# A hybrid decoder layer on one core: three rows of the tokens' fourth factor are loaded into the places of the blocks' transposed rows

## The chip, the core and the metric

The kernel runs on one core of one Trainium2 chip. Its metric is the device time of one execution in microseconds (us). Three runs of the kernel before gave 2222.38, 2222.5 and 2226.02 us; their median is 2222.5 us. The profile shows one further execution, with a time of its own.

## The reference

One decoder layer over 2048 tokens and 16 meta tokens, model width 1024, all in float32: an input projection, two groups of heads side by side (attention in a sliding window of 128, and a gated linear attention in chunks), an output projection, a layer norm, a SwiGLU feed-forward of width 2816, and a second layer norm.

```python
def hybrid_mixer(h, w_in, b_in, ...):
    proj = jnp.einsum('bld,de->ble', h, w_in) + b_in
    ...
    o_s = sliding_window_gqa(...)
    ...
    o_g = rms_norm(o_g, gla_norm_g).reshape(B, L, GLA_WIDTH) * jax.nn.silu(r_g)
    o = jnp.concatenate([o_s, o_g], axis=-1)
    return jnp.einsum('ble,ed->bld', o, w_out)

def reference(...):
    ...
    for l in range(DEPTH):
        mix = hybrid_mixer(h, ...)
        h = layer_norm(ALPHA * h + mix, ln1_g[l], ln1_b[l])
        ffn = swiglu(h, w_ffn_gate[l], w_ffn_up[l], w_ffn_down[l])
        h = layer_norm(ALPHA * h + ffn, ln2_g[l], ln2_b[l])
    return h[:, N_META:]
```

## The kernel before

Every matrix product of float32 values is made of three matmuls in a shorter format: an operand is split into a high part (a copy on ACT, L185) and a low part (a subtraction on DVE or POOL, L186), and TensorE (PE) adds high x high, low x high and high x low (`matmuls`, L197). `split_into` and `matmuls` are helpers, so many different steps of the program share these three lines; the tiles' names tell them apart.

The tokens are worked on in four blocks of 512 (s = 0 to 3). Each block is projected, mixed (attention and gated linear attention) and then given its output projection by the class `Mixed`. That class has the steps the change touches:

- `x(qd)`, four times per block, is a quarter of the output projection (256 columns). Its weights come as two loads of 1 MB, `hl_o{s}_{qd}_0` and `_1` (L221), and they go in turn through four places (tag "whl"). For each of the block's four groups of 128 tokens (n = 0 to 3) 24 matmuls write `po{s}_{n}_{qd}` into a PSUM bank, of which this step has two (tag "mm"). DVE then adds the bank to the residual row `yo{s}_{n}` (L930) and so frees the bank. The four residual rows are loaded by L915, 512 KB each, into seven places (tag "yo"): two blocks need eight, so `yo3_3`, the last row of the last block, takes the place of `yo2_0`, the first row of the block before, and can be loaded only when that row has been read for the last time.
- `y` is the layer norm of the rows and their store (L936). `z` transposes the finished rows on PE, eight transposed tiles per block, `nt{s}_{k}`, of four 128x128 transposes each (L943). ACT copies each one to a tile `ntr{s}_{k}` (L950, 256 KB, three places, tag "nt" in the pool `op_`), and it is stored to the scratch tensor `n_scT` (L952). The last transpose that reads `yo2_0` is the first of `nt2_7`.

The feed-forward works with sums of blocks ("factors") and seven products. The tokens' factors of the first half of the tokens are named by `EARLY = ["b11", "t2", "t1", "b21"]`, and those after it. `combine` makes the sums from `n_scT` and stores them in `t_sc` (its tiles `cb` take the places "nt" too); `make` loads a factor's four rows and splits them. A row is 128x512, 256 KB. `b11` and `t2` are made early, in the last block's steps; `t1` and `b21` are made once the projection's pools are closed (`ops.update({f: make(f, 0) ...})`). Their rows `r_t1..` and `r_b21..` go through three places, tag "mk" in the pool `hop1`, which they share with the rows of the next factor `t3`.

All of these steps end in one stretch, from some 876 us of the profile on: the matmuls of the last block's output projection (`po3_..`), the transposes of block 2 (`nt2_..`) and the loads of `t1`, `b21` and `t3` are laid out there by `FIRST_PRODUCTS`. The order of instructions on each engine is not written by hand: the framework's scheduler sets it with a simulation of its own when the kernel is built, from which buffers it believes to be free when. Every engine then runs its list strictly in order. SP issues nearly all DMAs, in its own order, on one hardware queue (q1), and with eight semaphores in turn: an issue also waits until the DMA eight issues before it has landed. In what follows, "SP" is this issuing engine.

Of the kernel before, what the change touches and what calls it, by code (L numbers as in the profile page):

```python
# [8 lines left out]
F32 = mybir.dt.float32  # L9
# [5 lines left out]
P = 128  # L15
# [108 lines left out]
def body(ctx, tc, t, seq):  # L124
# [11 lines left out]
    HT = TF // 2  # L136
# [47 lines left out]
    def split_into(hi, lo, src, lo_eng=None, hold=lambda i: i):  # L184
        hold(nc.scalar.activation(hi, src, AF.Copy))  # L185
        hold((lo_eng or nc.vector).tensor_tensor(lo, src, r32(hi), op=ALU.subtract))  # L186
# [18 lines left out]
    def staging(name):  # L205
        return wpool.tile([P, D], F32, tag="x", name=name, bufs=3)
# [68 lines left out]
    with ExitStack() as c1:  # L275
# [436 lines left out]
        for s in range(NSB):  # L712
# [5 lines left out]
            for what in WINDOW_STEPS.split():  # L718
                op, k = what[0], int(what[1])
# [26 lines left out]
    EARLY = ["b11", "t2", "t1", "b21"]  # L746
# [4 lines left out]
    pools = {}  # L751

    def quarter(tb, kh, th, k, n):

        c = tb * TF + th * HT
        k0 = kh * (KT // 2) + k
        return n_scT[c // TB][:, k0 : k0 + n, c % TB : c % TB + HT]
# [42 lines left out]
    def make(f, tb):  # L800

        if f in FIRST:
            x = hb.tile([P, 2, KT // 2, HT], F32R, tag="h16", name=f"h_{f}_{tb}", bufs=2)
        else:
            pool = pools["hop1" if f in EARLY else "hop3" if f == "b22" else "hop2"]
            x = pool.tile([P, 2, KT // 2, HT], F32R, tag=f"h_{f}", name=f"h_{f}_{tb}", bufs=1)
        if f in FIRST and tb == 0:
            for k in range(0, KT // 2, 2):
                raw = staging(f"r_{f}{tb}_{k}").rearrange("p (k q) -> p k q", q=HT)
                if f in SOURCE:  # L810
                    nc.sync.dma_start(raw, quarter(tb, *SOURCE[f], k, 2))
                else:
                    i, j = COMBINED[f]
                    nc.sync.dma_start(raw, t_sc[tb][i, :, k : k + 2, j])
                split_into(x[:, 0, k : k + 2], x[:, 1, k : k + 2], raw, nc.vector)
            return x
        if tb > 0:

            for k in range(0, KT // 2, 2):
                raw = pools["hop4"].tile([P, D], F32, tag="x3", name=f"r_{f}{tb}_{k}", bufs=4).rearrange("p (k q) -> p k q", q=HT)  # L820
                if f in SOURCE:
                    held(nc.sync.dma_start(raw, quarter(tb, *SOURCE[f], k, 2)))
                else:
                    i, j = COMBINED[f]
                    held(nc.sync.dma_start(raw, t_sc[tb][i, :, k : k + 2, j]))
                split_into(x[:, 0, k : k + 2], x[:, 1, k : k + 2], raw, nc.vector if k else nc.gpsimd)
            return x
        for k in range(KT // 2):
            raw = pools["hop1"].tile([P, HT], F32, tag="mk", name=f"r_{f}{tb}_{k}", bufs=3)
            if f in SOURCE:  # L830
                nc.sync.dma_start(raw, quarter(tb, *SOURCE[f], k, 1)[:, 0, :])
            else:
                i, j = COMBINED[f]
                nc.sync.dma_start(raw, t_sc[tb][i, :, k, j])
            split_into(x[:, 0, k], x[:, 1, k], raw, nc.vector if k % 2 else nc.gpsimd)
        return x
# [3 lines left out]
    op_ = c1.enter_context(tc.tile_pool(name="go", bufs=1, side="right", reuse_waits="tile"))  # L840
# [362 lines left out]
    def start_ffn(n):  # L1203

        if n < 2:
            ops[FIRST[n]] = make(FIRST[n], 0)
        elif n == 2:
            st = staging("a11_first")
            nc.sync.dma_start(st, t["w_gu"][0, 0, 0])
            hl = early["pa11"] = wpool.tile([P, 2, D], F32R, tag="whl", name="pa11_first", bufs=4)  # L1210
            split_into(hl[:, 0, :], hl[:, 1, :], st)
        else:
            hl = early.pop("pa11")
            early["b11"] = [mm_psum(f"b11{m}_first") for m in range(2)]
            for m, pt in enumerate(early["b11"]):
                matmuls(pt, ffn_terms(hl, ops["b11"], m))
# [33 lines left out]
    fp = hops.enter_context(tc.tile_pool(name="fp", bufs=1, reuse_waits="tile"))  # L1250
    pools["hop1"] = hops1.enter_context(tc.tile_pool(name="hop1", bufs=1, reuse_waits="tile"))
    ops.update({f: make(f, 0) for f in EARLY if f not in ops})


# [81 lines left out]
    raw, factors = {}, {}  # L1336
# [258 lines left out]
    AFTER, f = {}, None  # L1595
    for what in FIRST_PRODUCTS.split():
        if what[0] == "P":
            f = EARLY[int(what[1])]
# [4 lines left out]
    def finish_mixing(f):  # L1603
        for what in AFTER.get(f, ()):
            take(what.lower(), last if what[0] in "YZ" else mix)
        if f != BEFORE[-1]:
            return
        c1.close()
        pools["psB"] = hops.enter_context(tc.tile_pool(name="psB", bufs=1, space=PSUM, reuse_waits="tile"))
        for n in ("hop2", "hop3"):  # L1610
            pools[n] = c2.enter_context(tc.tile_pool(name=n, bufs=1, side="right", reuse_waits="tile"))
        ops.update({f: make(f, 0) for f in ("t3", "t4", "b22")})
        pools["hop4"] = hops1.enter_context(tc.tile_pool(name="hop4", bufs=1, reuse_waits="tile"))
# [132 lines left out]
```

## Time and profile before

| | |
|---|---|
| median of three runs | 2222.5 us (2222.38 to 2226.02) |
| the profiled execution's own time | 2216.87 us |
| its span | 2215.0 us |
| PE busy | 2158.8 us, 97% |
| DVE, POOL, ACT busy | 65%, 55%, 38% |

The profile is of one execution. Its own time is 1.87 us above its span and 5.63 us below the median of the three runs; a change of time is worked out inside this execution and then set on the median. PE is the busy engine, so a time is gained or lost where PE stands still, or where its clock is lowered: PEclk in a table of stretches is the granted clock as a share of the full 2.4 GHz, and 0.50 is 1.2 GHz. In a timeline a bracket at the end of a row tells how long the engine stood before that instruction and which instruction released it.

### The profile page before, as it was taken

The page shows a single profiled execution, that of the slowest core. Times are in us where ns is not written, and L with a number is a line of the kernel's source. Part 1 is how long each engine was busy: PE and PEld are TensorE (multiplying, and loading weights), DVE is VectorE, ACT ScalarE, POOL GpSimd, SP SyncE. Part 2 cuts the span into 40 slices and gives each one's busy share as a digit, 9 for nine tenths or more (in the row PEclk, how much of TensorE's full clock was granted, in tenths as well). Part 3 has the DMA queues.
Part 4 walks back from the last instruction along what each step waited for, and adds up shares of the span by engine and source line. Part 5 has one row for each costly group of instructions (what it writes and reads, how often), then busy time and mean ns, then how long its engine had stood idle before and what let it go on. Part 6 is the DMA issues. An engine that isn't in the chain of part 4 may idle for free.

```text
span 2215.0 us, 31559 instructions
## 1 busy us (share of the span) xinstructions
PE 2158.8 (97%) x11564; PEld 1858.7 (84%) x11564; DVE 1444.7 (65%) x2285; ACT 838.1 (38%) x1477; POOL 1220.2 (55%) x951
## 2 busy tenths in 40 slices
PE   8899999999999999999999999999999999999998
PEld 7788888889999998878888888788888888888886
DVE  6556645466745576368998567766656555876787
ACT  5544644544352443342223223322223242232443
POOL 4656645655634071368776666776666536432433
PEclk9999999999999999999999999999999999999999
DMA  8987773576786787766352318523232299655463
GB/s 296 316 277 252 254 268 127 193 277 226 290 294 225 253 310 244 274 252 219 130 196 103 131 45 286 189 101 109 90 125 81 98 360 330 219 185 177 166 232 124
DMA packets 181918, 460.92 MB, mean 208 GB/s; under 512 B 16978, under 2 KB 65011, under 8 KB 167684
## 3 DMA queue, kind: packets, MB, share of 16 engines
q1 hardware_dynamic: 176804, 452.26, 58.1%
q10 hardware_dynamic: 4960, 6.65, 0.8%
q8 instruction: 92, 1.51, 0.3%
q14 instruction: 62, 0.51, 0.1%
HBM read 306.67 MB, written 152.17 MB: 207 GB/s over the span
## 4 chain that ended last, share of the span: by engine, by line
PE 85%; DMA 4%; DVE 4%; POOL 3%; issue 2%; ACT 2%; SPq 0%; DVEq 0%; POOLq 0%; ACTq 0%
PE t L197 20%; PE d L1377 18%; PE b L197 14%; PE pu L197 13%; PE po L197 6%; PE pv L197 4%; PE lp L1151 2%; PE oa L680 1%; DMA r_t<-t_sc 1%; DMA cb<-n_scT 1%; DMA x<-x 1%; PE s L627 1%; PE s L628 1%; ACT pr L643 1%; PE nt L943 1%
## 5 line engine op out<-in xcount | busy, mean ns | idle before, releaser
L1377 PE MATMUL d<-B,A 128*128 128x512 f32 x1848 | 419.0, 389 | 0.0
L1377 PEld LDWEIGHTS d<-B,A 128*128 128x128 f32 x1848 | 346.9, 188 | 72.0
L197 PE MATMUL t<-h_t,ps 128*128 128x512 f32 x1584 | 367.9, 390 | 3.2 <-DMA ps<-parts_ps 2.4
L197 PEld LDWEIGHTS t<-h_t,ps 128*128 128x128 f32 x1584 | 296.8, 188 | 65.8 <-issue 2.1
L197 PE MATMUL pu<-h,hl_u 128*128 128x512 f32 (+1 forms) x1032 | 249.3, 389 | 7.2 <-ACT gr L692 4.5
L197 PE MATMUL b<-h_b,pa 128*128 128x512 f32 x1032 | 241.9, 390 | 0.3 <-ACT pa L185 0.2
L197 PEld LDWEIGHTS b<-h_b,pa 128*128 128x128 f32 x1032 | 193.7, 188 | 41.3 <-ACT pa L185 0.7
L186 POOL TENSOR_TENSOR pa<-a,pa 128x1024 fp32r<-128x1024 f32 x62 | 160.7, 2591 | 103.8 <-ACT pa L185 103.8
L197 PEld LDWEIGHTS pu<-h,hl_u 128*128 128x128 f32 x1032 | 184.0, 197 | 38.8 <-ACT gr L692 5.1
L197 PE MATMUL po<-hl_o,msh 128*128 128x256 f32 x1024 | 198.3, 289 | 4.8 <-DVE yo L930 3.1
L186 DVE TENSOR_TENSOR A<-rA,A 128x1024 fp32r<-128x1024 f32 (+1 forms) x78 | 117.2, 1527 | 119.7 <-ACT A L185 119.7
L197 PEld LDWEIGHTS po<-hl_o,msh 128*128 128x128 f32 x1024 | 162.1, 191 | 6.6 <-DVE yo L930 4.2
L185 ACT ACTIVATE A<-rA 128x1024 fp32r<-128x1024 f32 (+1 forms) x78 | 78.6, 1042 | 215.2 <-PE d L1377 200.2
L197 PE MATMUL po<-hl_o,msl 128*128 128x256 f32 x512 | 146.3, 286 | 0.0
L1647 DVE TENSOR_TENSOR u<-u,t 128x512 f32<-128x512 f32 x132 | 89.3, 680 | 84.2 <-PE t L197 84.1
L197 PE MATMUL b<-h_b,ps 128*128 128x512 f32 x528 | 126.9, 396 | 2.9 <-ACT h_b L185 2.8
L197 PE MATMUL t<-h_t,pa 128*128 128x512 f32 x528 | 123.8, 390 | 0.0
L1573 POOL TENSOR_TENSOR a<-a,a 128x1024 f32<-128x1024 f32 x42 | 121.2, 2887 | 1.6
L197 PEld LDWEIGHTS b<-h_b,ps 128*128 128x128 f32 x528 | 100.8, 191 | 25.0 <-ACT h_b L185 3.2
L197 PEld LDWEIGHTS t<-h_t,pa 128*128 128x128 f32 x528 | 99.0, 188 | 20.4
L185 ACT ACTIVATE ps<-a 128x1024 fp32r<-128x1024 f32 x63 | 66.7, 1059 | 123.4 <-PE t L197 81.9
L185 ACT ACTIVATE pa<-a 128x1024 fp32r<-128x1024 f32 x62 | 65.8, 1060 | 110.1 <-PE t L197 52.7
(355 smaller groups left out, 4292.0 us busy)
## 6 DMA issues: line engine op xcount, KB each, us to landing
hl_u<-w_u SPq DMA_DIRECT2D x42, 1024.0 KB, 6.7
a<-w_gu SPq DMA_DIRECT2D x84, 512.0 KB, 4.2
rA<-a_sc SPq DMA_DIRECT2D x66, 512.0 KB, 4.6
w<-w_d SPq DMA_DIRECT2D x50, 512.0 KB, 5.5
hl_o<-w_o SPq DMA_DIRECT2D x24, 1024.0 KB, 8.0
hT_sc<-h SPq DMA_DIRECT2D x32, 512.0 KB, 6.0
gh<-hT_sc SPq DMA_DIRECT2D x16, 1024.0 KB, 10.5
w_u<-hl_u SPq DMA_DIRECT2D x14, 1024.0 KB, 8.3
```

Of the source, the lines that this page charges most:

```text
L185: hold(nc.scalar.activation(hi, src, AF.Copy))
L186: hold((lo_eng or nc.vector).tensor_tensor(lo, src, r32(hi), op=ALU.subtract))
L197: last = hold(nc.tensor.matmul(out, l, r, start=(i == 0), stop=(i == n - 1)))
L627: nc.tensor.matmul(sp[:, :272], q, khh[:, hh, w], start=True, stop=False)
L628: nc.tensor.matmul(sp[:, :272], q, kll[:, hh, w], start=False, stop=True)
L643: nc.scalar.activation(pr[:, n, x, :], pr[:, n, x, :], AF.Exp, bias=nm[:, n, x : x + 1], scale=SLOPES[c0 + x // 2 + 4 * (x % 2)], accum_ou ...
L680: nc.tensor.matmul(oa[:, n], l, m, start=False, stop=(hh == 1 and i == 5))
L943: nc.tensor.transpose(tp[:, n, :], self.ys[n][:, k * P : (k + 1) * P], ident)
L1151: nc.tensor.matmul(o[:, P * j : P * j + P], kl[:, j, :], x[:, :, j, :], start=True, stop=True)
L1377: nc.tensor.matmul(pt, a_[:, a, ca], fb[:, b, cb], start=(p == 0 and j == 0), stop=(p == NP - 1 and j == 2))
L1573: sub = lambda o, x, y: nc.gpsimd.tensor_tensor(o, x, y, op=ALU.subtract)
L1647: nc.vector.tensor_tensor(o[i], x[i], y[i], op=ALU.add)
```

## The change

For the first three rows of `b21` (the fourth entry of `EARLY`) the tile is taken from the pool `op_` with the tag "nt", the three places that held the `cb` tiles before and that hold the transposed rows `ntr2_..` after; the fourth row keeps "mk". The two added lines shift all later line numbers by two. No instruction is added or removed.

```diff
--- before.py
+++ after.py
@@ -826,7 +826,9 @@
                 split_into(x[:, 0, k : k + 2], x[:, 1, k : k + 2], raw, nc.vector if k else nc.gpsimd)
             return x
         for k in range(KT // 2):
-            raw = pools["hop1"].tile([P, HT], F32, tag="mk", name=f"r_{f}{tb}_{k}", bufs=3)
+
+            pool, tag = (op_, "nt") if f == EARLY[3] and k < 3 else (pools["hop1"], "mk")
+            raw = pool.tile([P, HT], F32, tag=tag, name=f"r_{f}{tb}_{k}", bufs=3)
             if f in SOURCE:
                 nc.sync.dma_start(raw, quarter(tb, *SOURCE[f], k, 1)[:, 0, :])
             else:
```

With other places the scheduler lays the list of every engine out anew around these loads. Three places of the two lists that matter are shown: the names carry the factor or the block, then the row, and a number that only tells tiles apart.

SP before, from the load `cb0_3_10`, the last that `combine` makes; the rows of `b21` come some 30 issues later:

```order
L763 DMA cb0_3_10_8944<-n_scT0_62 128x512
L814 DMA r_t20_2_9715<-t_sc0_66 128x2x512
L1209 DMA a11_first_9827<-w_gu 128x1024
L897 DMA gm3_0_9994<-mS_sc_169 128x1024
L773 DMA t_sc0_66<-cb0_3_10_8944 128x512
L221 DMA hl_o2_3_0_9832<-w_o0_3_0_6713 128x2048
L897 DMA gm3_1_9998<-mS_sc_169 128x1024
L905 DMA gg3_0_10002<-mG_sc12_165 128x512
```

SP in the change, from the same load:

```order
L763 DMA cb0_3_10_8944<-n_scT0_62 128x512
L833 DMA r_b210_0_10073<-n_scT0_62 128x512
L814 DMA r_t20_2_9715<-t_sc0_66 128x2x512
L1211 DMA a11_first_9827<-w_gu 128x1024
L899 DMA gm3_0_9994<-mS_sc_169 128x1024
L773 DMA t_sc0_66<-cb0_3_10_8944 128x512
L833 DMA r_b210_1_10077<-n_scT0_62 128x512
L221 DMA hl_o2_3_0_9832<-w_o0_3_0_6713 128x2048
L899 DMA gm3_1_9998<-mS_sc_169 128x1024
L833 DMA r_b210_2_10081<-n_scT0_62 128x512
```

`r_b21` 0, 1 and 2 now stand 1, 6 and 9 places behind it, and the rows of `t2` and of the first weights `a11_first` are one place further back.

SP before, from the second weights of the third quarter on:

```order
L221 DMA hl_o3_2_1_10386<-w_o0_2_1_6602 128x2048
L831 DMA r_b210_2_10081<-n_scT0_62 128x512
L952 DMA n_scT2_64<-ntr2_3_10125 128x512
L831 DMA r_b210_3_10085<-n_scT0_62 128x512
L952 DMA n_scT2_64<-ntr2_4_10249 128x512
L834 DMA r_t30_0_10827<-t_sc0_66 128x512
L952 DMA n_scT2_64<-ntr2_5_10257 128x512
L915 DMA yo3_3_10134<-h_sc_60 128x1024
L221 DMA hl_o3_3_0_10492<-w_o0_3_0_6713 128x2048
```

SP in the change, from the same load:

```order
L221 DMA hl_o3_2_1_10386<-w_o0_2_1_6602 128x2048
L836 DMA r_t30_1_10831<-t_sc0_66 128x512
L836 DMA r_t30_2_10835<-t_sc0_66 128x512
L954 DMA n_scT2_64<-ntr2_3_10125 128x512
L954 DMA n_scT2_64<-ntr2_4_10249 128x512
L954 DMA n_scT2_64<-ntr2_5_10257 128x512
L221 DMA hl_o3_3_0_10492<-w_o0_3_0_6713 128x2048
L221 DMA hl_o3_3_1_10494<-w_o0_3_1_6720 128x2048
L917 DMA yo3_3_10134<-h_sc_60 128x1024
```

The loads of `r_b21` are gone from here and two of `t3` have come; `yo3_3` stood ahead of both loads of the last quarter's weights, `hl_o3_3_0` and `hl_o3_3_1`, and now stands behind them.

PE before, around the last transposed tile of block 2, whose first transpose is the last reader of `yo2_0`:

```order
L197 MATMUL po3_2_1_10332<-hl_o3_1_1_10278,msl3_9993 128x256
L197 MATMUL po3_2_1_10332<-hl_o3_1_1_10278,msh3_9992 128x256
L943 MATMUL nt2_7_10268<-ident_170,yo2_0_9266 128x128
L943 MATMUL nt2_7_10268<-ident_170,yo2_1_9268 128x128
L943 MATMUL nt2_7_10268<-ident_170,yo2_2_9270 128x128
L943 MATMUL nt2_7_10268<-ident_170,yo2_3_9272 128x128
L197 MATMUL po3_3_1_10358<-hl_o3_1_0_10276,msh3_9992 128x256
```

PE in the change:

```order
L197 MATMUL po3_3_1_10358<-hl_o3_1_1_10278,msl3_9993 128x256
L197 MATMUL po3_3_1_10358<-hl_o3_1_1_10278,msh3_9992 128x256
L945 MATMUL nt2_7_10268<-ident_170,yo2_0_9266 128x128
L945 MATMUL nt2_7_10268<-ident_170,yo2_1_9268 128x128
L945 MATMUL nt2_7_10268<-ident_170,yo2_2_9270 128x128
L945 MATMUL nt2_7_10268<-ident_170,yo2_3_9272 128x128
L197 MATMUL po3_0_2_10388<-hl_o3_2_0_10384,msh3_9992 128x256
```

The four transposes have moved from ahead of the 24 matmuls of `po3_3_1` to behind them. So has `nt2_5`, from ahead of `po3_2_1` to behind it.

## Rows read from the trace of the kernel before

**Rows 1.** The page: busy time, share of the span, instructions per engine.

```profile
PE 2158.8 (97%) x11564; PEld 1858.7 (84%) x11564; DVE 1444.7 (65%) x2285; ACT 838.1 (38%) x1477; POOL 1220.2 (55%) x951
```

**Rows 2.** PE's waits, 790 to 1000 us: total, times, longest.

```profile
PE po L197 <- DVE yo L930: 3.1, 2, 2.6
PE b L197 <- ACT h_b L185: 2.8, 1, 2.8
...
PE po L197 <- DMA hl_o<-w_o: 1.5, 1, 1.5
PE ot L1190 <- ACT ogn L1187: 1.2, 1, 1.2
```

**Rows 3.** Stretches of 10 us: PE, PEld, DVE, ACT, POOL, PEclk, DMA share, GB/s.

```profile
880.00:890.00 10.00, 9.85 (x74) 9.21 (x72) 4.16 (x8) 5.02 (x8) 2.07 (x3) 1.00 1.00 378
890.00:900.00 10.00, 8.04 (x66) 7.84 (x67) 2.41 (x5) 2.94 (x5) 5.79 (x3) 1.00 1.02 410
900.00:910.00 10.00, 9.33 (x75) 8.66 (x74) 3.83 (x6) 3.96 (x7) 4.50 (x3) 1.00 1.03 405
910.00:920.00 10.00, 7.39 (x62) 7.18 (x61) 1.87 (x4) 2.51 (x4) 1.30 (x1) 1.00 0.94 335
```

**Rows 4.** The chain that ended last, 860 to 1000 us: start, duration, what.

```profile
889.11 10.05 DMA hl_o<-w_o
...
908.41 0.24 PE po L197 x2
908.78 5.57 DMA yo<-h_sc
914.43 0.43 DVE yo L930
```

**Rows 5.** The timeline of PE, end of po3_3_1 and start of po3_0_2.

```profile
908.48 0.60 PE L943 MATMUL nt<-ident,yo 128*128 128x128 f32 x4
...
912.01 0.28 PE L197 MATMUL po<-hl_o,msh 128*128 128x256 f32 x1
914.90 0.38 PE L197 MATMUL po<-hl_o,msh 128*128 128x256 f32 x1 [2.61 <-DVE yo L930]
```

**Rows 6.** SP's timeline: DMA issues from 876 to 918 us.

```profile
891.70 0.32 SPq L831 DMA_DIRECT2D r_b<-n_scT  x1
...
903.45 0.32 SPq L831 DMA_DIRECT2D r_b<-n_scT  x1
...
908.78 0.32 SPq L915 DMA_DIRECT2D yo<-h_sc  x1
910.89 1.76 SPq L221 DMA_DIRECT2D hl_o<-w_o  x2
```

**Rows 7.** The page's DMA issues: KB each, median us to landing.

```profile
a<-w_gu SPq DMA_DIRECT2D x84, 512.0 KB, 4.2
```

**Rows 8.** ACT's timeline, 840 to 862 us.

```profile
854.14 1.06 ACT L185 ACTIVATE pa_first<-a_first 128x1024 fp32r<-128x1024 f32 x1 [1.57 <-DMA a_first<-w_gu]
```

**Rows 9.** PE's waits, 100 to 125 us.

```profile
PE pu L197 <- ACT gr L692: 3.4, 1, 3.4
```

**Rows 10.** PE after that wait, by 1 us: busy, PEclk, DMA share, GB/s.

```profile
112.00:113.00 1.00, 1.00 (x3) 0.50 1.17 401
113.00:114.00 1.00, 1.00 (x4) 0.50 1.06 328
114.00:115.00 1.00, 1.00 (x4) 0.53 1.04 381
```

**Rows 11.** PE around 971.9 us, by 2 us, same columns.

```profile
972.00:974.00 2.00, 1.86 (x4) 0.50 1.01 334
974.00:976.00 2.00, 2.00 (x7) 0.50 1.02 404
976.00:978.00 2.00, 2.00 (x6) 0.50 0.73 270
978.00:980.00 2.00, 2.00 (x9) 0.87 0.03 10
```

## The prediction

> **What bounds the kernel now.** I read the busy shares first, then the waits of PE in the region that the change rearranges, then the stretches there, then the chain of waits, and last the timelines of PE and SP. PE is busy for 97% of the span [rows 1], so time is won or lost only where PE stands. The waits name those places [rows 2]: twice PE waits for DVE's work on a residual row `yo` (3.1 us, the longer one 2.6), once 1.5 us for weights `hl_o`, once 1.2 us for `ogn`, and once 2.8 us for ACT's `h_b`, some 60 us later. The first two belong to a stretch with one property: from 880 to 910 us the DMA engines are busy all the time, at 378, 410 and 405 GB/s [rows 3], 398 on average. While that lasts, a transfer lands when the bytes ahead of it are through, and moving 1 MB ahead of it costs about 2.6 us.
>
> The chain shows whom this hurts [rows 4]. The weights `hl_o3_1_1` are issued at 889.11 and take 10.05 us. Then PE works without much of a gap until the load of `yo3_3`, issued at 908.78, landing 5.57 us later, at 914.35; DVE takes it up at 914.43. Why does PE wait for it? The step has two PSUM banks, and `po3_3_0` and `po3_3_1` both hold one until DVE has added them to `yo3_3`. So `po3_0_2` has no bank: PE ends `po3_3_1` at 912.01 + 0.28 = 912.29 and starts again at 914.90, 2.61 us later [rows 5]. The time at which PE goes on is set by one 512 KB load.
>
> **The change, part by part.** No operation is added, so every term is a place in a queue.
>
> *Relief.* The three rows of `b21` were issued from 891.70 to 903.45 [rows 6], in the full stretch. In the change the first goes out ahead of `a11_first`, which ACT had by 854.14 [rows 8], and the others few places behind it: some 40 us earlier. That takes 3 x 262 KB = 0.79 MB from the queue, 2.0 us at 398 GB/s. Their splits on ACT, POOL and DVE move with them; these engines are free for about half of each 10 us there, or more [rows 3], so I cost the splits at nothing. `hl_o3_1_1` gets an earlier place and PE's 1.5 us for it [rows 2] should mostly vanish. Against that, `nt2_5` no longer stands ahead of `po3_2_1`, so the wait for the one rotating bank, 3.1 - 2.6 = 0.5 us at the other `po` [rows 2], comes a second time. By these terms PE would end `po3_3_1` near 912.29 - 1.5 + 0.5 - 0.4 = 910.9; the 0.4 is `nt2_7` (most of its 0.60 us [rows 5], pipelined), which follows instead of preceding.
>
> *The late row.* None of that reaches the end, because PE must still wait for `yo3_3`, and this load is moved back. Its place is free only after the first transpose of `nt2_7`. That was at 908.48, ahead of `po3_3_1`; it is now behind it. On SP the load was ahead of `hl_o3_3_0` and `hl_o3_3_1`; now it is behind both, and the second of these waits for the end of `po3_3_1`, which is the last to read the weights whose place it takes (before, both issues stretch over 1.76 us from 910.89 [rows 6]). Bytes ahead of `yo3_3`, against before: minus three rows of `b21` (-0.79 MB), plus two rows of `t3` (+0.52), plus two weight loads (+2.10) = +1.84 MB, or 4.6 us at 398 GB/s. It lands near 919 instead of 914.35. The 10 us from 910 moved only 335 GB/s [rows 3], which is because the queue runs short between issues; 0.4 us of the delay may be absorbed by such gaps, as bytes ahead then move in time that was lost before. I take **+4.2 us**.
> The ends: if the load were held up only by its issue, at about 911.3, and landed as a load of that size does in the median of the weights `a`, 4.2 us [rows 7], it would be there at 915.5, PE would go on 0.55 us later as now, and the term is +1.1. At 335 GB/s the same bytes take 5.5 us: +5.5. I am nearer the upper end, since the queue is full in the rows of this very stretch.
>
> *The clock.* PE would stand from about 911 to 919, some 8 us. After the wait of 3.4 us near the start [rows 9] the granted clock was 0.50, 0.50 and 0.53 in the three following us [rows 10]: 0.50 + 0.50 + 0.47 = 1.5 us of full-speed work lost. After the 2.8 us wait for `h_b` it was 0.50 for 6 us and 0.87 for the next 2 [rows 11]: 3 x 1.0 + 0.26 = 3.3 us lost. After the 2.61 us wait of today there is no such loss: PE's clock reads 1.00 in all stretches of [rows 3]. With a wait three times as long I expect 1.2 GHz for some us after it. I take the middle of the two, **+2.4 us**; the ends are 0 and 3.3.
>
> *The first weights.* The row `r_b21_0` now stands ahead of `r_t2` and `a11_first`. ACT waited 1.57 us for `a11_first`, until 854.14 [rows 8], and PE's wait for `ogn`, 1.2 us, hangs on ACT there [rows 2]. One row more in front is at most 262 KB / 398 GB/s = 0.65 us and, where the queue is idle, nothing. I take **+0.2**.
>
> What follows the matmuls of `po3` is paced by PE or runs after it; the later wait for `h_b` moves along, since the loads and splits behind it are released by work that moves with PE. I give it nothing, 0 to -3.3 if its clock drop did not recur.
>
> Sum: +4.2 + 2.4 + 0.2 = **+6.8 us**. The profiled execution would go from 2216.87 to 2223.7; it is 5.6 us below the median of the runs, so on the median 2222.5 becomes **2229.3 us**. A measurement of this kernel tells about 0.2%, 4.4 us: slower begins at 2226.9, faster ends at 2218.1.
>
> The Trainium skill ("DMA: Bandwidth & Descriptors", section "Anatomy of one DMA — SWDGE (gpsimd) path") gives a fit of about 2.0 us plus the bytes over 436 GB/s for one DMA, which for 512 KB is an estimate of 3.2 us; it is fitted to DMAs issued by another engine. By it alone the late row would cost about +0.1 us; the trace disagrees, with 5.57 us for this load today.
>
> **The rivals.**
>
> *The queue decides less than the bytes say.* The load of `yo3_3` lands about 4.2 us after its issue, the +1.1 above, the clock costs 0 to 1.5, the first weights 0.2: +1.3 to +2.8, some 2225. For it: the median of [rows 7], and the queue's shares below 1 after 910 [rows 3]. Against it: `hl_o3_1_1`, with no more ahead of it than this load will have, took 10.05 us [rows 4]. That is the case in which the fit of the skill would be the better guide. Chance 0.18.
>
> *Faster: the relief reaches the end.* The 2.0 us of traffic taken away make `yo3_3` land before PE needs its bank, and the waits of `po` go: 3.1 + 1.5 us [rows 2] = 4.6 us, 2222.5 - 4.6 = 2217.9. This decides if the load lands before about 911, which needs an issue before some 906. For it: the DMA is the full resource here, and it is relieved. Against it: the order of both lists, in which the load cannot be issued before the end of `po3_3_1`. Chance 0.08.
>
> *Nothing is seen.* The early rows cost the earlier stretch what they save here, and the late row is covered by another 1 or 2 us of the relief than I count; 2220 to 2225, centre 2222.5. Or the rows would not be loaded earlier at all; the list of SP speaks against that. Chance 0.11.
>
> *Worse.* The shift lets PE's clock fall a second time, or the late queue delays the rows of `t3`, which are wanted next: +9 to +14, some 2234. Chance 0.07.
>
> **How the numbers follow.** The forecast has 0.56. Its own range is from +1.1 + 1.5 to +5.5 + 3.3 + 0.65, that is 2225 to 2232. Of it about nine tenths lie over 2226.9. Slower: 0.56 x 0.9 + 0.07 + a sixth of the first rival = 0.60. Faster: the second rival, 0.08. Same: the rest, 0.32. The range must take in most of the first rival and of the third: 2221.5 to 2233.
>
> **What would show it.** In the profile of the changed kernel: SP issues three `r_b` before 860 us; the wait for `hl_o` is gone; the load of `yo` stands after two of `hl_o` on SP and lands 6 to 8 us after its issue; PE has a wait of 6 to 9 us "for DVE yo" near 911 to 919, and PEclk at 0.50 after it. I am wrong if that wait is under 4 us, if PEclk stays 1.00, or if the difference comes from behind the last `po3`, where I expect only a shift.

## The result and the profile after

The change made the kernel slower: 2227.63 us, the median of 11 runs (2224.86 to 2232.45), against 2222.38 us, the median of 11 runs of the kernel before on the same chip (2217.15 to 2226.02). The ratio of the two sets of runs is 1.003, with a 95% interval of 1.0021 to 1.004; on 2222.5 us that is +6.7 us, between +4.7 and +8.9. The two medians by themselves are 5.25 us apart. The forecast was +6.8 us. One execution of run 2 below took 4376.67 us, against 2215.8 to 2221.25 for its other ten, and is left out of its ratio.

The profiled execution of the change has a span of 2223.0 us, 8.0 more than that of before. Both executions are among the shortest of their kernels: 2224.86 us is the lowest of the 11 runs of the change, and 2216.87 us lies below all 11 of before.

The waits of PE from 790 to 1010 us, in total, times and longest, answer to [rows 2]:

```profile
PE po L197 <- DVE yo L932: 9.8, 3, 8.8
PE b L197 <- ACT h_b L185: 2.8, 1, 2.8
...
PE po L197 <- DMA hl_o<-w_o: 0.3, 1, 0.3
```

The longest wait for the row `yo` has grown from 2.6 to 8.8 us. The wait for `ogn` is gone, and so is the 1.5 us wait for `hl_o`: the 0.3 us in the last row is a wait at another place, ahead of the stretch, where the kernel before had none. PE's timeline before, and that of the change:

```profile
899.21 0.39 PE L197 MATMUL po<-hl_o,msh 128*128 128x256 f32 x1 [1.55 <-DMA hl_o<-w_o]
```

```profile
866.55 0.38 PE L197 MATMUL po<-hl_o,msh 128*128 128x256 f32 x1 [0.34 <-DMA hl_o<-w_o]
```

The chain that ended last shows why the wait for `yo` has grown, where [rows 4] stood:

```profile
909.37 0.44 PE nt L945 x4
909.82 8.22 DMA yo<-h_sc
918.13 0.43 DVE yo L932
918.61 22.74 PE po L197 x168
```

The load of `yo3_3` starts right behind the four transposes of `nt2_7` and takes 8.22 us instead of 5.57; PE goes on at 918.61 instead of 914.90. The 168 matmuls from there on take 22.74 us. The same piece of the chain before:

```profile
914.90 20.41 PE po L197 x168
```

22.74 - 20.41 = 2.33 us is what the lowered clock costs. SP's timeline shows what was issued ahead of the row:

```profile
844.44 0.32 SPq L833 DMA_DIRECT2D r_b<-n_scT  x1
...
848.68 0.50 SPq L833 DMA_DIRECT2D r_b<-n_scT  x1
...
854.57 0.32 SPq L833 DMA_DIRECT2D r_b<-n_scT  x1
...
907.96 1.76 SPq L221 DMA_DIRECT2D hl_o<-w_o  x2
909.82 0.39 SPq L917 DMA_DIRECT2D yo<-h_sc  x1
```

The three rows `r_b` go out at 844, 849 and 855 us, as the built list had it, and at 908 two loads `hl_o` of 1 MB each go ahead of the row. The stretches of 10 us, with the columns of [rows 3], show both sides of the trade:

```profile
890.00:900.00 10.00, 9.49 (x80) 9.28 (x79) 2.84 (x5) 2.20 (x4) 7.80 (x4) 1.00 1.03 403
900.00:910.00 10.00, 9.30 (x77) 8.85 (x75) 2.14 (x4) 3.07 (x6) 0.02 (x1) 1.00 1.04 393
910.00:920.00 10.00, 1.39 (x6) 1.39 (x7) 0.75 (x2) 1.32 (x2) 0.00 (x0) 0.69 0.79 300
920.00:930.00 10.00, 10.00 (x71) 10.00 (x70) 0.97 (x3) 0.00 (x0) 0.00 (x0) 0.80 0.01 2
```

From 890 to 900 PE now works 9.49 us where it worked 8.04: that is the relief. From 910 to 920 it works 1.39 us where it worked 7.39. The stretches of 1 us, with the same columns, show the clock:

```profile
912.00:913.00 1.00, 0.00 (x0) 0.00 (x0) 0.00 (x0) 0.00 (x0) 0.00 (x0) 1.00 0.69 262
913.00:914.00 1.00, 0.00 (x0) 0.00 (x0) 0.00 (x0) 0.00 (x0) 0.00 (x0) 0.85 1.04 418
914.00:915.00 1.00, 0.00 (x0) 0.00 (x0) 0.00 (x0) 0.00 (x0) 0.00 (x0) 0.50 0.96 369
...
920.00:921.00 1.00, 1.00 (x7) 1.00 (x6) 0.00 (x0) 0.00 (x0) 0.00 (x0) 0.50 0.00 0
...
923.00:924.00 1.00, 1.00 (x7) 1.00 (x6) 0.00 (x0) 0.00 (x0) 0.00 (x0) 0.53 0.00 0
924.00:925.00 1.00, 1.00 (x11) 1.00 (x11) 0.42 (x1) 0.00 (x0) 0.00 (x0) 1.00 0.00 0
```

PE ended `nt2_7` at 909.81. The granted clock falls to 0.50 (1.2 GHz) during the wait itself, within the us from 913, and stays there until 923 to 924, five us after PE has gone on.

Single executions differ by some us before this region is reached, so for comparing traces I use one distance within each: from the first matmul of `b_first` to the last transpose of the last block, `nt3_7`. The two tile views of before give its ends (first and last start stand behind the durations):

```profile
L197 PE MATMUL b_first<-h_b,pa_first x24: 389/390/477, 876.3 to 881.8; 128*128 128x512 f32 x24
```

```profile
L943 PE MATMUL nt<-ident,yo x64: 270/272/328, 876.1 to 968.3; 128*128 128x128 f32 x64
```

That is 968.3 - 876.3 = 92.0 us. The same two rows of the change:

```profile
L197 PE MATMUL b_first<-h_b,pa_first x24: 387/391/482, 875.7 to 881.4; 128*128 128x512 f32 x24
```

```profile
L945 PE MATMUL nt<-ident,yo x64: 270/272/328, 878.5 to 974.5; 128*128 128x128 f32 x64
```

974.5 - 875.7 = 98.8 us, 6.8 more. "The distance" below is this one. The region holds the loss that the runs show; what the one profiled span shows above it (8.0 against 6.8) lies in other places of the program, and I don't count it to the change. The distance leaves out what stands ahead of `b_first`, where the rows of `b21` now are. From 790 us to there PE's waits add up to 4.4 us before and 4.7 in the change; over the runs below they are 2.6 to 6.3 us with three early rows and 2.7 to 4.8 with fewer, so these traces would not show a cost of the early rows there that is smaller than this spread.

### The profile page after: what moved, and what is told of

The parts are those of the page before. It is cut to its first block, busy times and chain, and to the rows that moved or that the text cites. A ratio compares the mean times of both kernels' runs of the same rounds, so it can differ in the third digit from the quotient of the medians.

```text
span 2223.0 us, 31553 instructions
## 1 busy us (share of the span) xinstructions
PE 2159.1 (97%) x11564; PEld 1857.6 (84%) x11564; DVE 1445.4 (65%) x2285; ACT 836.7 (38%) x1477; POOL 1220.2 (55%) x951
## 4 chain that ended last, share of the span: by engine, by line
PE 83%; DVE 6%; DMA 4%; POOL 2%; ACT 2%; issue 2%; SPq 0%; DVEq 0%; POOLq 0%; ACTq 0%
PE t L197 20%; PE d L1379 17%; PE b L197 14%; PE pu L197 12%; PE po L197 7%; PE pv L197 3%; PE lp L1153 2%; PE oa L680 1%; DMA cb<-n_scT 1%; PE nt L945 1%; PE s L627 1%; PE s L628 1%; DMA ps<-parts_ps 1%; DVE A L186 1%; ACT pr L643 1%
## 5 line engine op out<-in xcount | busy, mean ns | idle before, releaser
L186 DVE TENSOR_TENSOR ps<-a,ps 128x1024 fp32r<-128x1024 f32 x42 | 75.2, 1790 | 50.6 <-ACT ps L185 50.6
```

## The experiments

The theory: the loss is one late load, through a held PSUM bank, and the clock that falls while PE stands. Its rivals: the early rows cost something by being early, or only the whole new order counts. "Before" in a ratio is the kernel before, run beside each on the same chip.

| run | ratio to before, 95% interval | PE's wait for `yo3_3`, us | 168 matmuls, us | distance, us |
|---|---|---|---|---|
| before | | 2.61 | 20.41 | 92.0 |
| the change | 1.003 (1.0021 to 1.004) | 8.80 | 22.74 | 98.8 |
| 1, `nt2_7` first | 0.9996 (0.9986 to 1.0006) | 3.98 | 23.14 | 94.9 |
| 2, row first on SP | 0.9994 (0.9985 to 1.0003) | 3.77 | 21.88 | 92.7 |
| 3, before with `nt2_7` late | 1.0029 (1.0017 to 1.0042) | 8.34 | 22.15 | 98.6 |
| 4, 60 transposes in the wait | 1.0028 (1.0016 to 1.0039) | 2.73 left | 21.90 | 98.3 |
| 5, one row | 0.9996 (0.9984 to 1.0007) | 2.67 | 21.75 | 92.5 |
| 6, two rows | 1.0013 (1.0005 to 1.0022) | 4.98 | 22.27 | 95.5 |
| 7, 84 transposes in the wait | 1.0023 (1.0015 to 1.0032) | 0.49 left | 20.42 | 97.3 |
| 8, row first and 33 transposes | 1.0003 (0.9994 to 1.0012) | 0.76 left | 20.42 | 91.9 |
| 9, the change, quarter put off | 0.9981 (0.997 to 0.9992) | none of its own | not comparable | 88.8 |
| 10, before, quarter put off | 0.9989 (0.9979 to 0.9998) | none of its own | not comparable | 89.8 |
| 11, one row, quarter put off | 0.9989 (0.9979 to 0.9999) | none of its own | not comparable | 89.1 |

**1. `nt2_7` ahead of `po3_3_1` again, all else as in the change.** In step `x`, for the last block:

```diff
-                matmuls(pt[:, :256], terms)
+                behind = tc.issue_after(early["nt"].ins) if (s, qd, n) == (NSB - 1, 1, 3) else ExitStack()
+                with behind:
+                    matmuls(pt[:, :256], terms)
...
```

> The change with its three early rows, and one pin: the matmuls of po3_3_1 are queued behind the transposes of nt2_7 on PE, as before. The lists then have the load of yo3_3 ahead of both hl_o3_3 loads again. Theory (the late row): the 8.8 us wait shrinks to 2 to 4 us, PEclk stays near 1.00, and the time is 5 to 8 us under the changed kernel, that is 0 to 3 us under the kernel before, ratio 0.9985 to 1.000. Rival (the early loads themselves, or the relocated splits, cost the time): it stays within 2 us of the changed kernel, ratio 1.002 or more.

The ratio came to 0.9996, so the loss is gone with this one pin, and the early rows stay. The rival that they cost the time falls. The clock was a miss: PE waited 3.98 us and then ran at 0.50 for some us (23.14 us for the 168 matmuls), which I had expected to stay near 1.00:

```profile
910.40 6.56 DMA yo<-h_sc
...
917.52 23.14 PE po L197 x168
```

Counted from `b_first` (878.8), PE was done with `po3_3_1` after 34.7 us, 1.3 earlier than before (36.0), but the row landed after 38.2, as before (38.0): with neither weight load ahead of it, it still took 6.56 us. So in this execution nothing of the relief reached the row. The execution, at 2223.73 us, was the slowest of the 11 runs (median 2218.71), and its distance, 94.9, does not show what the ratio of all of them shows.

**2. SP's order alone restored.** `nt2_7` stays late, but the last quarter's weights are queued behind the row:

```diff
-            hl = [unit(t["w_o"][qd, q], ...) for q in range(2)]
+            behind = tc.issue_after(self.load.ins) if (s, qd) == (NSB - 1, 3) else ExitStack()
+            with behind:
+                hl = [unit(t["w_o"][qd, q], ...) for q in range(2)]
```

> The change, with SP's order alone restored: both hl_o3_3 loads queued behind the load of yo3_3; nt2_7 stays behind po3_3_1 on PE. Theory (2 MB in the queue ahead of the row is most of the delay): issue near 909.5, landing 4 to 5 us later, the wait is 4 to 5 us instead of 8.8, ratio to the kernel before 0.999 to 1.001. Rival (the late issue alone is the delay, not what is in the queue): the row still lands near 917, the wait is over 7 us and the ratio 1.002 or more.

The row is issued at 909.35, at nearly the same place as in the change (909.82), and lands 3.52 us later and not 8.22, as the chain shows:

```profile
909.35 3.52 DMA yo<-h_sc
...
913.42 21.88 PE po L197 x168
```

The two weight loads now go out behind the row:

```profile
909.73 0.90 SPq L221 DMA_DIRECT2D hl_o<-w_o  x2
```

So of the 5.1 us between the landings of run 2 and of the change (37.3 against 42.3 us from `b_first`), 4.7 are the 2 MB ahead in the queue and 0.4 the issue. The late place on PE is not free: the issue is 1.3 us later than before (33.8 against 32.5 us from `b_first`), and the quicker landing, 3.52 us in place of 5.57, makes up for it. The ratio is 0.9994 as expected. One thing is to be seen here: PE goes on 37.8 us after the start of `b_first` (875.6), 0.8 earlier than before (38.6), and then loses 21.88 - 20.41 = 1.5 us to the clock. In this execution the relief was there, and the clock took it back.

**3. The kernel before, with `nt2_7` late and no row moved.** The transposed tile 7 is made in a step of its own after `x1`:

```diff
-FIRST_PRODUCTS = "P0 Z0 x0 Z1 x1 x2 x3 y0 P1 z0 P2 z1 P3"
+FIRST_PRODUCTS = "P0 Z0 x0 Z1 x1 Z2 x2 x3 y0 P1 z0 P2 z1 P3"
...
-            for k in range(4 * k2, 4 * k2 + 4):
+            for k in ([7] if k2 == 2 else [4, 5, 6] if (s, k2) == (NSB - 2, 1) else range(4 * k2, 4 * k2 + 4)):
...
+                behind = tc.issue_after(early["po", NSB - 1, 1, 3].ins) if k2 == 2 else ExitStack()
```

> The kernel before, all four rows of b21 where they were, with one pin: nt2_7 is queued behind po3_3_1 on PE. SP's list then has the load of yo3_3 behind both hl_o3_3 loads, as in the change. Theory: the row lands about 5 us later than 914.35, the clock falls to 1.2 GHz, the time rises by 5 to 8 us, ratio 1.002 to 1.004, as in the change, without any early row. Rival (the early rows are the cause): within 1 us of the kernel before, ratio 0.9995 to 1.0005.

It is the whole loss without the change: ratio 1.0029, distance 98.6 against 98.8. The chain has the same link as that of the change, a row behind two weight loads, and the slower matmuls. The issue of the weights, from SP's timeline, and the chain:

```profile
913.24 1.76 SPq L221 DMA_DIRECT2D hl_o<-w_o  x2
```

```profile
915.10 7.74 DMA yo<-h_sc
...
923.43 22.15 PE po L197 x168
```

The row landed 42.8 us after the start of `b_first` (880.0), 4.8 later than before (38.0). Of these, 2.6 us are the later issue (35.1 against 32.5) and 2.2 the longer landing (7.74 against 5.57) with 2.1 MB more ahead of it.

**4 and 7. Work for PE inside the wait.** In the change, the transposes of `nt2_7` for the groups 1 to 3 are repeated 20 times, and 28 times in run 7; they write the same values again:

```diff
+                for n in [1, 2, 3] * (20 if (s, k) == (NSB - 2, 7) else 0):
+                    nc.tensor.transpose(tp[:, n, :], self.ys[n][:, k * P : (k + 1) * P], ident)
```

> The change, with the transposes of nt2_7 for the groups 1 to 3 repeated 20 times, 60 more transposes of some 0.11 us, about 6.6 us of work inside the 8.8 us wait; the results are the same. Theory (the clock falls because PE stands): PE goes on at about the same time, 918 to 919, PEclk stays 1.00 behind it, and the time is 2 to 3 us under the changed kernel, ratio to the kernel before 1.001 to 1.002. Rival (the clock falls for another reason, or the delay is all of the loss): no gain, ratio 1.003, or more by the added work.

> As the run with 60 more transposes, with 84, some 9.1 us of work: what is left of the wait should be under 1 us. Theory (PE standing lets the clock fall): PEclk 1.00 until the step's end, the 168 matmuls from po3_0_2 on take 20.4 us as before and not 22.7, and from b_first to the last nt it is 96 to 97 us; ratio to the kernel before 1.0015 to 1.0025. Rival (the clock falls all the same, as behind the 2.73 us that were left in the run with 60): 21.5 to 23 us for the 168 matmuls.

With 60 transposes I missed: they ended 2.73 us before the row came, the clock fell in that rest, and the 168 matmuls took 21.90 us. The stretches of 2 us (busy PE, PEclk, DMA share, GB/s) show the clock at 1.00 through the work and falling in the gap behind it:

```profile
916.00:918.00 2.00, 2.00 (x21) 1.00 0.98 354
918.00:920.00 2.00, 0.47 (x5) 1.00 0.86 343
920.00:922.00 2.00, 0.80 (x3) 0.79 0.39 146
922.00:924.00 2.00, 2.00 (x11) 0.50 0.00 0
```

With 84 a wait of 0.49 us was left, PEclk stayed 1.00 and the 168 matmuls took 20.42 us, as before:

```profile
910.00:912.00 2.00, 2.00 (x21) 1.00 0.89 351
...
918.00:920.00 2.00, 1.51 (x13) 1.00 0.03 11
920.00:922.00 2.00, 2.00 (x19) 1.00 0.35 131
```

The distance is 97.3, 1.5 less than that of the change. So the clock falls because PE stands, and it can be kept with work that is of no use. The ratio, 1.0023, has an interval that overlaps that of the change; on the run's time alone the gain is not shown.

**5 and 6. One and two rows in place of three** (`k < 1` and `k < 2` in the line of the change).

> The change for one row of b21 only (k < 1). The lists keep nt2_7 ahead of po3_3_1 and the load of yo3_3 ahead of both hl_o3_3 loads. Theory (only the late row costs): no loss, 0 to 1 us gained by 0.26 MB less in the full stretch; from the first matmul of b_first to the last transpose nt 91 to 92.5 us (before 92.0, the change 98.8); ratio 0.999 to 1.0005. Rival (each early row costs by itself, about a third of the loss): ratio 1.001, 94 us.

> The change for two rows (k < 2). The lists have nt2_7 inside po3_3_1 and the load of yo3_3 between hl_o3_3_0 and hl_o3_3_1: 1 MB ahead of the row and not 2. Theory: the row lands about 2 us later than before, the wait is 4 to 6 us, the clock falls to 1.2 GHz for some us; from b_first to the last nt 94 to 96 us, ratio 1.001 to 1.002. Rival (the order counts only as a whole): as the changed kernel, 98 to 99 us, or as before, 92.

One row moves nothing of the order around `yo3_3`, and the ratio is 0.9996. With two, the row goes between the two weight loads, as SP's timeline shows, 1 MB ahead of it and not 2:

```profile
910.49 0.32 SPq L221 DMA_DIRECT2D hl_o<-w_o  x1
911.44 0.32 SPq L917 DMA_DIRECT2D yo<-h_sc  x1
912.36 0.32 SPq L221 DMA_DIRECT2D hl_o<-w_o  x1
```

The wait is 4.98 us, the distance 95.5, the ratio 1.0013: a loss between nothing and that of three rows, so the order does not count only as a whole. It goes with the row's place in the order, not with the number of rows moved, since one row costs nothing. That the 1 MB ahead delays it is not shown by this run: the row took 5.30 us (911.44 to 916.74), which lies within the 3.52 to 6.56 of the kernel before and of runs 1, 2, 5 and 8 to 10, with neither weight load ahead of it. It landed 1.6 us later than before (39.6 against 38.0 us from `b_first`) because it was issued 1.8 us later (34.3 against 32.5), behind `nt2_7`. With both loads ahead (the change, runs 3, 4 and 7) it took 7.74 to 9.08.

**8. Row first on SP, and 33 transposes in what is left of the wait.**

> The change with SP's order restored (the load of yo3_3 ahead of both hl_o3_3 loads) and 33 more transposes, some 3.6 us, in the 3.77 us wait that was left there. Theory (there the fallen clock alone gives back what the early rows win): PEclk stays 1.00, the 168 matmuls take 20.4 us and not 21.9, from b_first to the last nt 91 us against 92.0 before and 92.7 with the order alone; ratio 0.998 to 0.9995. Rival (the early rows win nothing at the end): 92 us or more, ratio 0.9995 to 1.0005.

The clock stayed at 1.00 and the matmuls took 20.42 us, but the distance was 91.9 and the ratio 1.0003: no gain that can be measured. Of the two steps expected one came. From PE's going on to the last transpose it was 53.4 us, as before, and 54.9 in run 2: the clock's 1.5 us are won. But PE went on 38.5 us after `b_first`, 0.7 later than in run 2 (37.8) and as late as before (38.6), because the row, in the same order on SP, took 4.10 us here and 3.52 there. What made this load slower is not shown.

**9, 10 and 11. The bank is not held.** `po3_3_1` is put off behind `po3_0_2`, so that while the row is on its way PE has 24 other matmuls, whose bank does not hang on that row. In step `x`:

```diff
+            todo = [(qd, n, hl) for n in range(NB)]
+            if s == NSB - 1 and qd == 1:
+                self.put_off = todo.pop()
+            if s == NSB - 1 and qd == 2:
+                todo.insert(1, self.put_off)
...
-            for n in range(NB):
+            for qd, n, hl in todo:
+                cs = slice(256 * qd, 256 * qd + 256)
```

> The change with the three early rows, and the matmuls of po3_3_1 put off behind those of po3_0_2, so that the second bank is not held while the row is on its way. The lists then have nt2_7 ahead of po3_0_2 and the load of yo3_3 ahead of both hl_o3_3 loads. Theory (the bank held for the late row is the wait; the early rows do relieve the stretch): no wait over 1 us at this place, PEclk 1.00, from b_first to the last nt 88 to 90 us (before 92.0), ratio to the kernel before 0.998 to 0.9992. Rival (the wait only changes its name: po3_0_2 now waits for hl_o3_2, or po3_0_3 for hl_o3_3, whose places come free 3 us later): a wait of 2 to 4 us for DMA hl_o, 91.5 to 93 us, ratio 0.9995 to 1.0005.

> The kernel before with po3_3_1 put off in the same way, no row moved. Theory: the 2.61 us wait goes, from b_first to the last nt 89 to 90.5 us, ratio 0.9985 to 0.9995; against the run of the change with the same step it is 0.5 to 1.5 us slower, which is what the early rows are worth. Rival (as there): a wait for hl_o in its place, 91.5 to 93 us.

> One early row (k < 1) with po3_3_1 put off. Theory: between the two others, 88.5 to 90 us from b_first to the last nt, ratio 0.998 to 0.9993. Rival: as for the others.

The intervals of all three ratios end below 1, two of them by 0.0001 and 0.0002 only, and the run with the three early rows has the shortest distance: 88.8 us, against 89.8 without an early row and 89.1 with one. Run 9's waits from 876 to 945 us are three for the rotating bank, 0.51 us each, and a short one for `ntr`:

```profile
PE po L197 <- DVE yo L937: 1.5, 3, 0.5
PE nt L950 <- ACT ntr L957: 0.5, 1, 0.5
```

SP issues the row far ahead of the weights, which now wait for the later end of `po3_3_1`:

```profile
907.95 0.38 SPq L917 DMA_DIRECT2D yo<-h_sc  x1
...
913.33 0.32 SPq L221 DMA_DIRECT2D hl_o<-w_o  x1
...
914.77 0.32 SPq L221 DMA_DIRECT2D hl_o<-w_o  x1
```

No wait for weights has taken its place, and PE stays at its clock (columns of [rows 3]):

```profile
900.00:910.00 10.00, 9.01 (x75) 8.57 (x74) 2.25 (x5) 3.49 (x5) 0.61 (x1) 1.00 1.02 396
910.00:920.00 10.00, 9.49 (x80) 9.28 (x79) 1.69 (x4) 1.45 (x2) 0.00 (x0) 1.00 0.76 272
920.00:930.00 10.00, 10.00 (x86) 10.00 (x85) 5.47 (x11) 3.06 (x3) 2.96 (x2) 1.00 0.11 43
```

In run 10, without early rows, the wait for `hl_o` is still there:

```profile
PE po L197 <- DMA hl_o<-w_o: 1.5, 1, 1.5
PE po L197 <- DVE yo L935: 1.0, 2, 0.5
```

Of the 1.0 us between the two distances, 0.5 is PE's waits in the stretch (2.55 us in run 10, 2.01 in run 9): the 1.5 for `hl_o`, less one more wait for the rotating bank and the one for `ntr`. The rest is about what other work in the stretch takes: run 10 has 96 matmuls of the product `t` between the two ends, run 9 has 94, and one takes some 0.23 us. So what the change is worth here, once nothing behind it takes it back, is about 0.5 us in these two traces. As times the two don't part: 0.9981 (0.997 to 0.9992) and 0.9989 (0.9979 to 0.9998) overlap.

## Why the prediction was right

- **The late row.** Forecast: the load behind two of `hl_o`, +4.2 us. It was issued behind them, and PE went on 3.7 us later, or 4.3 later counted from `b_first` (42.9 against 38.6 us). Of the 4.3 us, 1.6 are the later issue (34.1 against 32.5 us from `b_first`) and 2.65 the longer landing (8.22 against 5.57; the forecast had 6 to 8 us from issue to landing), which the forecast's sum of bytes did not part. That the 2 MB ahead delay the row is shown by run 2 against the change, the same loads in another order: 4.7 us. Bytes do not tell the whole: with neither weight load ahead the row took anything from 3.52 to 6.56 us, so that 4.2 came so near to 4.3 is in part luck. The Trainium skill ("DMA: Bandwidth & Descriptors", section "Anatomy of one DMA — SWDGE (gpsimd) path") gives a fit by which 512 KB would take an estimate of 3.2 us; run 2, with 174 and 269 GB/s in the two stretches of 2 us from 908 to 912, is near it with 3.52, and the change is not, with 8.22. The section is about DMAs that GpSimd issues, and this load is issued by SP.
- **The clock.** Forecast +2.4 us, a middle between two rows of other places; measured 22.74 - 20.41 = 2.33. That PE standing is the cause is shown by runs 7 and 8. The two rows, 1.5 and 3.3, stood for waits of 3.4 and 2.8 us; the runs have 1.3 to 2.7 us for waits of 2.67 to 8.80, so the size of the wait does not set the size of the loss, and the middle was luck as much as reason. (The term named 0 as its low end, and the forecast's own range then used 1.5.)
- **The relief that reaches no end.** Forecast: the wait for `hl_o` mostly gone, PE early, and all of it swallowed by the row. The wait of 1.55 us is gone, in this trace and in all others with three early rows, and with fewer it is 0.9 to 1.5 us (runs 3, 5, 6, 10 and 11). PE ended `po3_3_1` and `nt2_7` at 909.81, earlier than the 910.9 that I had for `po3_3_1` alone. By runs 9 and 10 the relief is worth about 0.5 us of PE's waits, with one trace of each.
- **The first weights.** Forecast +0.2 us. The wait that the term was to lengthen did not come: ACT took `a11_first` at 853.08 without a wait (before at 854.14, after 1.57 us), and PE's wait of 1.2 us for `ogn` is gone. Other waits ahead of `b_first` are longer, and together they are 4.7 us against 4.4, so the sign of the term is open. It was small enough not to matter.
- **Behind the last `po3`.** Forecast: only a shift. From PE's going on to the last transpose it was 53.4 us before and 55.9 in the change, 2.5 more, of which 2.33 is the clock; the wait for `h_b` is 2.8 us in both, and the granted clock is 0.50 behind it in both. A further fall of the clock, which I had named as the worse case, is not there. With 4.3 us up to PE's going on, the 2.5 make the 6.8 of the distance.
- **The rivals.** That the queue would decide less than the bytes say is refuted by run 2 against the change, an issue half a us apart and a landing 5 us apart. "Nothing is seen" is refuted by the ratio. The faster case named its own condition, the row landing before PE needs its bank, and in the change that did not hold. Run 9 is another kernel, in which PE needs that bank later; it has 0.9981, about 4.2 us less than before.

## What to carry to other kernels

When a change frees a place for an early load, ask the scheduler's new lists which load has become late: here the cost was a 512 KB row that slipped behind 2 MB on one queue, and not anything that the change was about. Price a slipped load by its later issue and by the bytes now ahead of it at the rate the stretch shows, allow some us for what bytes don't explain, and add the clock where PE will stand for it. And before trimming the traffic, look at what is held while the load is on its way: one PSUM bank less held, by putting one group of matmuls off, took 2.7 us from PE's waits in this stretch (5.24 in the kernel before, 2.55 in run 10), and the traffic some 0.5 more.

## What was not expected

The granted clock fell during the wait, before PE went on: in the change between 913 and 914, with PE standing since 909.81. And it hangs on small differences: after 2.61 us without work, in the kernel before, there was no loss, and after 2.67 us in run 5 it fell and the 168 matmuls took 21.75 us instead of 20.41:

```profile
913.53 0.58 PE L197 MATMUL po<-hl_o,msh 128*128 128x256 f32 x1 [2.67 <-DVE yo L932]
```

Whether such a wait costs 0 or 1.3 us more cannot be read from its length alone in these runs.
